# A third raw weight buffer, bias tables by products, and carried states four at a time, in one decoder layer step on one core

## The chip, the cores and the metric

The kernel runs on one core of a Trainium2 chip. Its engines have queues of their own and wait for each other by semaphores: TensorE (PE for matmuls, PEld for its weight loads), VectorE (DVE), ScalarE (ACT), GpSimd (POOL) and SyncE (SP), which here issues most DMA transfers. The metric is the device time of one execution in microseconds (us). TensorE's clock has two levels here, 2.4 and 1.2 GHz; the profile gives the granted clock of a stretch as a share of the upper one (PEclk).

## The reference, cut to what matters

One decoder layer step for a prompt of 256 tokens and 8 samples of 8 tokens, 320 columns in all, in float32:

```python
x = x + 0.5 * swiglu_ffn(rmsnorm(x, ffn1_norm), ffn1_w_in, ffn1_w_out)
h = rmsnorm(x, mix_norm)
z, xbc, dt_raw, q, kv, nsa_g, merge_g = jnp.split(h @ w_in_proj, cuts, axis=-1)
# state-space mixer: per sample and group, with the carried state h0
y_off = jnp.einsum('bclgn,bcgjpn->bclgjp', Cc, h_start) * decay_from_start[..., None]
h_final, h_start = lax.scan(step, h0, ...)      # h * decay + new state
# attention: compressed, selected and window keys, each with a bias by distance
s_c = jnp.einsum('bthgd,bnhd->bthgn', q, kc) + bias_qk(dist_c, bias_tab)
m = sig(gA) * (y_ssd @ w_branch_ssm) + sig(gB) * (y_nsa @ w_branch_attn);  x = x + m @ w_out
x = x + 0.5 * swiglu_ffn(rmsnorm(x, ffn2_norm), ffn2_w_in, ffn2_w_out)
```

`bias_tab` holds one bias for each of 32 buckets of distance and 16 heads. The samples read 2048 past tokens from paged caches, whose compressed keys and values (`kc`, `vc`) are computed in this step. A carried state has 64 rows by 128 columns for each of 32 heads; a group of eight heads of one sample is a 128 x 512 tile here, so there are 8 samples x 4 groups = 32 such tiles.

## The kernel before, in words

**The dense stream.** All big products take their weights in 245 blocks of up to eight K tiles (128 rows each, 1928 tiles in all). `w_load` (L300 to L308) lets SP load a block of 512 KB into one of `NRAW` = 2 buffers `wraw`. `w_hi` (L314) has ACT cast it to the high part `wh`; `w_lo` (L323) has DVE take the rest as the low part `wl` and then issues the next `w_load`, since the raw buffer is free from there on. `dense` (L328) runs three products for each K tile (L342 high x high, L343 low x high, L344 high x low), casts the high part of a later block at the first K tile of a block and the low part at `k == 1`. SP's queue is in order: a weight load stands behind whatever was issued before it, and with a wait of its own.

**The side work.** After each K tile `Sched.tick` adds `RATE[stage]` to a credit and lets generators take steps with it, so everything else stands between the K tiles of the dense stream in an order that is fixed when the program is written. `wait(n)` lets n ticks pass; `S.defer(n, f)` runs f after n ticks, from the front of a list.

**The stages**, in the time of the profiled execution: 0 to 390 the first feed-forward block, with the compression of the cached pages (`cmp_stream`) at its side; from 390 the projection `wproj`, first with `cmp_keys` (L717), `prompt_bias` (L839) and the prompt's attention, then from about 690 with the state-space mixer (`prompt_chunks`, `sample_chunks` L1747); from about 890 the samples' attention (`sample_attn`, `ring` of seven `KV` buffers) beside the last projections and branches; from about 1150 the second feed-forward block, whose norm takes its sums of squares with `Squares` (L347, products at L392).

**Bias.** In `cmp_stream` eight products (L638) make the bias of every head and distance, which POOL writes to DRAM (`trev`). At the end of the first feed-forward block SP issues, in this order: `xsp`, the two loads of `w1c` (L830), `scv` (L1178), three weight blocks, then the four loads of `prompt_bias` from `trev` into `blob` (L847), `flip` (L849), and the two small tables `tb` and `cb` (L837) in 16 loads, those of `cb` with single elements of 4 bytes. The product L855 needs `blob` and `flip`; L733 transposes the keys that `cmp_keys` has scaled on DVE (L726, L727), after `wait(4)`. `positions` (L599 to L603) has 16 one-column products (L602) twice in the program.

**Carried states.** `load_h` (L1726) loads state j into a ring of `NH` = 6 buffers, `AHEAD` = 4 states before it is used. In `sample_chunks`, for each even sample b, two products (L1772, 32 output rows each, in neighbouring groups of 32 rows) multiply the states of b and b + 1 by `cz`; then, for each state, POOL multiplies it by its decay (L1775), two products (L1778, L1779) make the new part, DVE adds it (L1780), the store of the state before is issued and then the load of state j + 4. Two samples make one step.

## Time and profile before

| what | value |
|---|---|
| three timed runs | 1389.57, 1389.86 and 1399.72 us, median 1389.86 |
| the profiled execution | 1398.44 us |
| its span, first to last instruction | 1396.4 us |
| busy: PE, PEld, DVE, ACT, POOL | 1329.4, 1177.7, 866.0, 592.8, 363.5 us |
| mean granted clock of PE in the span | 0.961 |
| DMA | 251.66 MB, mean 180 GB/s |

Busy time is a share of one span over stages with different limits. PE's busy time holds what it loses at the lower clock: an instruction at 1.2 GHz counts with its longer time. A view of the chain of waits follows the last instruction back, at each step to what released it. The timeline gives each instruction's start and length, and in brackets the idle time before it and its releaser. Windows sum up stretches.

### The profile page before, as it was taken

How to read it: one execution, taken by the hardware profiler on the slowest of the kernel's cores; microseconds unless marked ns; L12 is line 12 of the kernel's file. 1: busy time of each engine (PE TensorE's matmuls, PEld its weight loads, DVE VectorE, ACT ScalarE, POOL GpSimd, SP SyncE). 2: the span in 40 equal slices, each digit the busy share in tenths (PEclk: the TensorE clock that was granted, in tenths of full speed). 3: DMA queues.
4: the chain of work that ended last, by engine and by line, in shares of the span. 5: the costliest groups of instructions: out<-in, count | busy, mean ns of one | idle time of the engine just before them, and what ended most of it. 6: DMA issues, size and time to landing. Idle time of an engine off the chain costs nothing.

```text
span 1396.4 us, 28186 instructions
## 1 busy us (share of the span) xinstructions
PE 1329.4 (95%) x10583; PEld 1177.7 (84%) x10583; DVE 866.0 (62%) x1862; ACT 592.8 (42%) x1152; POOL 363.5 (26%) x616
## 2 busy tenths in 40 slices
PE   8999999999979999889989989799999999999998
PEld 7899999999858878677877756577677999999998
DVE  5577656655556457866567657657767766666533
ACT  4454543445434324446544343255555344333322
POOL 2222212222000216554444435233340010000000
PEclk9999999999989999889999999999999999999999
DMA  7556656666544325421177686778894443444453
GB/s 258 164 192 201 221 184 198 210 205 201 209 100 126 125 96 198 182 91 61 50 197 214 190 237 181 290 249 314 267 333 148 168 140 134 149 149 151 148 171 110
DMA packets 107041, 251.66 MB, mean 180 GB/s; under 512 B 23208, under 2 KB 49849, under 8 KB 104953
## 3 DMA queue, kind: packets, MB, share of 16 engines
q1 hardware_dynamic: 89946, 198.27, 44.2%
q0 software_dynamic: 16960, 51.61, 11.1%
q8 instruction: 83, 1.36, 0.4%
q14 instruction: 52, 0.43, 0.1%
HBM read 235.11 MB, written 23.10 MB: 185 GB/s over the span
## 4 chain that ended last, share of the span: by engine, by line
PE 72%; DVE 11%; DMA 5%; issue 4%; ACT 4%; SPq 2%; POOL 1%; POOLq 0%; ACTq 0%; DVEq 0%
PE ps_pd L342 18%; PE ps_pd L343 16%; PE ps_pd L344 16%; DVE wl L323 3%; PE ps_sc L671 2%; PE ps_sc L672 2%; PE ps_sc L681 2%; ACT wh L314 2%; PE ps_sc L1431 2%; DVE cvo L1198 2%; PE ps_po L1471 1%; DMA out_ssmS<-h 1%; PE ps_pt L1457 1%; PE ps_po L1319 1%; PE ps_sc L1270 1%
## 5 line engine op out<-in xcount | busy, mean ns | idle before, releaser
L323 DVE TENSOR_TENSOR wl<-wraw,wh 128x1024 fp32r<-128x1024 f32 (+1 forms) x245 | 302.0, 1233 | 266.9 <-ACT wh L314 266.4
L342 PE MATMUL ps_pd<-hh,wh 128*128 128x320 f32 x1320 | 452.5, 343 | 4.5 <-ACT hh L751 1.8
L343 PE MATMUL ps_pd<-hl,wh 128*128 128x320 f32 x1320 | 418.0, 317 | 1.6 <-DVE hl L450 1.4
L344 PE MATMUL ps_pd<-hh,wl 128*128 128x320 f32 x1320 | 417.2, 316 | 0.0
L314 ACT CAST wh<-wraw 128x1024 fp32r<-128x1024 f32 (+1 forms) x245 | 252.7, 1031 | 167.2 <-PE ps_pd L343 125.0
L342 PEld LDWEIGHTS ps_pd<-hh,wh 128*128 128x128 f32 x1320 | 257.4, 195 | 44.6 <-issue 32.8
L343 PEld LDWEIGHTS ps_pd<-hl,wh 128*128 128x128 f32 x1320 | 257.6, 195 | 10.2 <-issue 5.3
L344 PEld LDWEIGHTS ps_pd<-hh,wl 128*128 128x128 f32 x1320 | 256.5, 194 | 0.0
L342 PE MATMUL ps_pd<-ah,wh 128*128 128x320 f32 x352 | 109.4, 311 | 0.0
L344 PE MATMUL ps_pd<-ah,wl 128*128 128x320 f32 x352 | 108.7, 309 | 0.0
L343 PE MATMUL ps_pd<-al,wh 128*128 128x320 f32 x320 | 98.7, 309 | 0.0
L563 POOL DMA_DIRECT2D pg<-in_cache x136 | 74.3, 547 | 73.6 <-DVE pgl L575 30.6
L235 POOL TENSOR_SCALAR ah<-ff 128x320 fp32r<-128x320 f32 x44 | 20.1, 458 | 277.9 <-DVE ff L478 277.8
L575 DVE TENSOR_TENSOR pgl<-pg,pgh 128x512 fp32r<-128x512 f32 x128 | 82.4, 685 | 15.1 <-ACT pgh L568 14.9
L1384 POOL DMA_DIRECT2D KV<-in_cache x102 | 55.0, 539 | 104.3 <-PE ps_po L1471 68.5
L473 ACT ACTIVATE sg<-sg 128x320 f32<-128x320 f32 x44 | 20.8, 472 | 135.1 <-DVE sg L472 135.0
L568 ACT CAST pgh<-pg 128x512 fp32r<-128x512 f32 x128 | 72.6, 616 | 9.0 <-PE ps_sc L672 7.3
L671 PE MATMUL ps_sc<-pgh,w1h 128*128 128x256 f32 x256 | 68.6, 289 | 2.5 <-ACT pgh L568 2.5
L672 PE MATMUL ps_sc<-pgh,w1l 128*128 128x256 f32 x256 | 68.6, 288 | 0.0
L342 PEld LDWEIGHTS ps_pd<-ah,wh 128*128 128x128 f32 x352 | 66.1, 188 | 0.5
L344 PEld LDWEIGHTS ps_pd<-ah,wl 128*128 128x128 f32 x352 | 66.1, 188 | 0.0
L343 PEld LDWEIGHTS ps_pd<-al,wh 128*128 128x128 f32 x320 | 60.2, 188 | 0.0
(453 smaller groups left out, 2250.2 us busy)
## 6 DMA issues: line engine op xcount, KB each, us to landing
wraw<-in_wproj SPq DMA_DIRECT2D x77, 512.0 KB
KV<-in_cache POOLq DMA_DIRECT2D x102, 256.0 KB, 5.4
wraw<-in_w1in SPq DMA_DIRECT2D x44, 512.0 KB
wraw<-in_w2in SPq DMA_DIRECT2D x44, 512.0 KB
pg<-in_cache POOLq DMA_DIRECT2D x136, 128.0 KB, 4.1
pg<-in_cache SPq DMA_DIRECT2D x120, 128.0 KB
wraw<-in_w1out SPq DMA_DIRECT2D x16, 512.0 KB
h<-in_ssm SPq DMA_DIRECT2D x32, 256.0 KB
```

Of the source, the lines that this page charges most:

```text
L314: a.copy(h[:, :n], st["raw"][i][:, :n])
L323: v.tensor_tensor(l[:, :n], st["raw"].pop(i)[:, :n], st["hl"][i][0][:, :n], op=ALU.subtract)
L342: pe.matmul(out, wh[:, s], xh[:, kk, :], start=kk == 0, stop=False)
L343: pe.matmul(out, wh[:, s], xl[:, kk, :], start=False, stop=False)
L344: pe.matmul(out, wl[:, s], xh[:, kk, :], start=False, stop=kk == K - 1)
L563: e.dma_start(page(s, half)[:, i, :], I["cache"][ds(r, 1), :, 256 * c : 256 * c + 256].rearrange("o p f -> p (o f)"))
L568: a.copy(h[:, 8 * half : 8 * half + 8, :], page(s, half)[:, :, 64 * q : 64 * q + 64])
L575: v.tensor_tensor(l[:, 8 * half : 8 * half + 8, :], page(s, half)[:, :, 64 * q : 64 * q + 64], h[:, 8 * half : 8 * half + 8, :], op=ALU.su ...
L671: pe.matmul(ph, wh[:, j, :], h[:, :, j, :], start=q + j == 0, stop=False)
L672: pe.matmul(ph, wl[:, j, :], h[:, :, j, :], start=False, stop=False)
L681: pe.matmul(ph, wh[:, j, :], l[:, :, j, :], start=False, stop=q + j == 6)
L1384: e.dma_start(t[:, j, :], I["cache"][ds(r, 1), :, 512:1024].rearrange("o p f -> p (o f)"))
```

## The change

Four things are changed, and some counts beside them.

1. Three raw weight buffers in place of two; the low part is issued at the third K tile of a block (`k == 2`). The DMA scratch is halved from 8192 to 4096.
2. `tb` and `cb` no longer come from `trev` by 16 loads. In `cmp_stream`, after the loop that makes `trev`, 24 products (one for each of eight tokens and three groups of columns: 8, 63 and 1) with 33 rows of weights add them up in one PSUM tile; `relz` is `rel` spread with zeros between. `flip` is loaded there too. The four loads of `blob` are issued before `w1c`; `scv` is loaded later, at the fifth block of the projection. `cmp_keys` waits seven ticks instead of four.
3. Four carried states are multiplied at once, for b = 0 and b = 4, from a ring of eight buffers, loaded five ahead; the load is issued before the store. `xl` has 128 rows instead of 64, so that L1779 (now L1788) reads them all. The first `stage_b` of the samples stands six ticks later; `RATE[4]` is 0.88 instead of 0.85. `WS`, the wait at the start of the samples' attention, is 4 instead of 8.
4. `defer` sorts its list by what is left to wait; the squares before the second feed-forward block are deferred by 5 instead of 3.

```diff
-W0, W1, W2, W3, WS, EB = 3, 3, 6, 1, 8, 2
+W0, W1, W2, W3, WS, EB = 3, 3, 6, 1, 4, 2
-RATE = (0.59, 1.2, 0.9, 1.5, 0.85, 1.0, 1.0)
+RATE = (0.59, 1.2, 0.9, 1.5, 0.88, 1.0, 1.0)
     def defer(self, n, f):
-        self.later.append([n, f])
+        i = len(self.later)
+        while i and self.later[i - 1][0] > n:
+            i -= 1
+        self.later.insert(i, [n, f])
-    NRAW, SA = 2, 2
+    NRAW, SA = 3, 2
-                if k == 1:
+                if k == 2:
                     w_lo()
...
+        gcopy(relz[:, 7::8][:, 0:16], rel[:, 0:16])
+
+        p = bank("sc", (128, 72))
+        last = lambda t: oht[:, 6 - t : 7 - t] if t < 7 else oh[:, 2047:2048]
+        for o, n, src in ((0, 8, lambda t: oht[:, 7 - t : 15 - t]), (8, 63, lambda t: oh[:, 38 - t : 2048 - t : 32][:, 0:63]),
+                          (71, 1, last)):
+            for t in range(T):
+                pe.matmul(p[:, o : o + n], relz[:, 7 - t : 135 - t], src(t), start=t == 0, stop=t == T - 1)
+        a.copy(kcv[:, 2048:2120], p)
         release("oh")
+        sp.dma_start(flip, I["con"][:, C_KEEP : C_KEEP + 128])
...
-        yield from wait(4)
+        yield from wait(7)
...
-        flip = st["blob"][:, 4600:4728]
-        sp.dma_start(flip, I["con"][:, C_KEEP : C_KEEP + 128])
-        load_bias(tb, PAST, 8)
-        load_bias(cb, 31, 64, 32)
...
-        NH, AHEAD = 6, 4
+        NH, AHEAD = 8, 5
...
-            xl = sx.tile([64, 512], F32R, tag="xl", bufs=1, name="xl")
+            xl = sx.tile([128, 512], F32R, tag="xl", bufs=1, name="xl")
...
+                if q == 0:
+                    yield from wait(6)
                 stage_b(q, 2)
...
-                    if b % 2 == 0:
-                        for x_ in range(2):
-                            r = 32 * ((b + x_) % 4)
-                            pe.matmul(py[r : r + 32, :], cz[:, b + x_, :], pend["h", j + x_], start=b + x_ < 4,
-                                      stop=b + x_ >= 4)
+                    if b % 4 == 0:
+                        for x_ in range(4):
+                            r = 32 * x_
+                            pe.matmul(py[r : r + 32, :], cz[:, b + x_, :], pend["h", j + x_], start=b == 0, stop=b == 4)
...
+                    load_h(j + AHEAD)
                     store("outH")
                     pend["outH"] = O["ssmS"][b, :, 512 * q : 512 * q + 512], h0
-                    load_h(j + AHEAD)
...
-    early = chain(cmp_keys(), prompt_bias(), selector(), until("gates"), both(gates_rows(), decays()))
+    bias_ = prompt_bias()
+    next(bias_)
+    for c in range(2):
+        sp.dma_start(w1b[:, c], I["w1c"][:, c])
+    early = chain(cmp_keys(), bias_, selector(), until("gates"), both(gates_rows(), decays()))
...
+        if i == 4:
+            sp.dma_start(scv, I["sconv"])
...
-    sq = Squares(8, 3)
+    sq = Squares(8, 5)
```

Where the instructions stand shows in the order on each queue. SP, at the border of the first feed-forward block and the projection, before (`xsp` keeps the residual, `w1t` is `w1c`'s place):

```order
L305 DMA wraw<-in_wproj 128x1024 x4
L778 DMA xsp<-x 128x2560
L830 DMA w1t<-in_w1c 128x2048 x2
L1178 DMA scv<-in_sconv 128x576
L305 DMA wraw<-in_wproj 128x1024 x3
L847 DMA blob<-trev 64x4x256 x4
L849 DMA blob<-in_con 128x128
L837 DMA tb<-trev 16x8 x8
L837 DMA cb<-trev 16x64x1 x8
```

and after the change:

```order
L308 DMA wraw<-in_wproj 128x1024 x4
L794 DMA xsp<-x 128x2560
L859 DMA blob<-trev 64x4x256 x4
L1863 DMA w1t<-in_w1c 128x2048 x2
L308 DMA wraw<-in_wproj 128x1024 x6
L901 DMA blob<-in_con 48x432
```

The loads of `blob` stand four places earlier, ahead of `w1c`; the 16 loads of the tables are gone, and `scv` and `flip` stand elsewhere.

PE in the first feed-forward block, at the last product that makes `trev` (L638), before:

```order
L638 MATMUL ps_sc<-oht,rel 32x72
L342 MATMUL ps_pd<-hh,wh 128x320
L343 MATMUL ps_pd<-hl,wh 128x320
L344 MATMUL ps_pd<-hh,wl 128x320
L342 MATMUL ps_pd<-hh,wh 128x320
```

and after the change, three K tiles of the dense stream behind that product (now L644):

```order
L345 MATMUL ps_pd<-hh,wh 128x320
L346 MATMUL ps_pd<-hl,wh 128x320
L347 MATMUL ps_pd<-hh,wl 128x320
L656 MATMUL ps_sc<-oht 128x8 x8
L656 MATMUL ps_sc<-pg_119,oht 128x63 x8
L656 MATMUL ps_sc<-oht 128x1 x7
L656 MATMUL ps_sc<-pg_119,oht 128x1
L345 MATMUL ps_pd<-hh,wh 128x320
```

The 24 products stand in one piece between two K tiles.

PE in the first group of carried states, before (`h0` the states, `ps_po` the output that all samples of a group share):

```order
L1772 MATMUL ps_po_8452<-h0_8141,cz_8133 32x512
L1772 MATMUL ps_po_8452<-h0_8143,cz_8133 32x512
L1778 MATMUL ps_sc_8456<-xh_8391,bz_8395 128x512
L1779 MATMUL ps_sc_8456<-xl_8392,bz_8395 128x512
L1778 MATMUL ps_sc_8463<-xh_8391,bz_8395 128x512
L1779 MATMUL ps_sc_8463<-xl_8392,bz_8395 128x512
L342 MATMUL ps_pd_8411<-hh_4690,wh_8314 128x320
L343 MATMUL ps_pd_8411<-hl_4691,wh_8314 128x320
```

and after the change:

```order
L1782 MATMUL ps_po_8631<-h0_8152,cz_8144 32x512
L1782 MATMUL ps_po_8631<-h0_8154,cz_8144 32x512
L1782 MATMUL ps_po_8631<-h0_8156,cz_8144 32x512
L1782 MATMUL ps_po_8631<-h0_8158,cz_8144 32x512
L1787 MATMUL ps_sc_8637<-xh_8536,bz_8540 128x512
L1788 MATMUL ps_sc_8637<-xl_8537,bz_8540 128x512
L1787 MATMUL ps_sc_8644<-xh_8536,bz_8540 128x512
L1788 MATMUL ps_sc_8644<-xl_8537,bz_8540 128x512
L345 MATMUL ps_pd_8615<-hh_4720,wh_8478 128x320
L346 MATMUL ps_pd_8615<-hl_4721,wh_8478 128x320
```

Four states stand in a row where there were two; the next four follow after the new parts of four states. SP in the same group, where the second four states are loaded, before:

```order
L305 DMA wraw_8369<-in_wproj 128x1024
L1581 DMA abs_8417<-ascr_80 64x8x64
L305 DMA wraw_8425<-in_wproj 128x1024
L1726 DMA h0_8460<-in_ssm 128x512
L1679 DMA out_ssmS<-h0_8141 128x512
L1726 DMA h0_8468<-in_ssm 128x512
L1679 DMA out_ssmS<-h0_8143 128x512
L1726 DMA h0_8487<-in_ssm 128x512
L1679 DMA out_ssmS<-h0_8145 128x512
L1726 DMA h0_8495<-in_ssm 128x512
```

and after the change:

```order
L308 DMA wraw_8629<-in_wproj 128x1024
L1733 DMA h0_8641<-in_ssm 128x512
L1733 DMA h0_8648<-in_ssm 128x512
L1686 DMA out_ssmS<-h0_8152 128x512
L1733 DMA h0_8662<-in_ssm 128x512
L1686 DMA out_ssmS<-h0_8154 128x512
L1733 DMA h0_8670<-in_ssm 128x512
L1686 DMA out_ssmS<-h0_8156 128x512
L1681 DMA ecb_8684<-ascr_80 64x4x128 x2
L1733 DMA h0_8706<-in_ssm 128x512
L1686 DMA out_ssmS<-h0_8158 128x512
L1733 DMA h0_8714<-in_ssm 128x512
```

The load of a state stands ahead of a store instead of behind it; states 6 and 7 of a group stand right before and right behind the first store.

## Rows read from the trace of the kernel before

**Rows 1.** The page, part 1: busy time, share and instructions of each engine.

```profile
PE 1329.4 (95%) x10583; PEld 1177.7 (84%) x10583; DVE 866.0 (62%) x1862; ACT 592.8 (42%) x1152; POOL 363.5 (26%) x616
```

**Rows 2.** Timeline of PE; in brackets idle time before, and its releaser.

```profile
395.58 1.11 PE L733 MATMUL ps_sc<-con,kcv 128*128 128x128 f32 x4 [2.45 <-DVE kcv L727]
...
411.84 2.05 PE L855 MATMUL ps_sc<-blob 128*128 128x512 f32 x2 [4.44 <-DMA blob<-in_con]
...
717.49 1.12 PE L1637 MATMUL ps_pt<-abs,xdt 64*64 64x64 f32 x16 [5.42 <-POOL abs L1627]
...
807.04 0.80 PE L1778 MATMUL ps_sc<-xh,bz 128*128 128x512 f32 x1 [4.42 <-ACT btok L1608]
...
902.60 1.06 PE L1431 MATMUL ps_sc<-KV,qbs 64*32 64x512 f32 x1 [5.97 <-DVE ms L1444]
...
1159.26 0.38 PE L392 MATMUL ps_pt<-ones,sq 128*128 128x1 f32 x2 [1.30 <-ACT sq L365]
```

**Rows 3.** Chain of waits, three windows: start, length, what.

```profile
404.55 7.21 DMA blob<-in_con
...
704.40 8.33 DMA wraw<-in_wproj
...
889.02 12.84 DMA KV<-in_cwin
```

**Rows 4.** Timeline of SP from 360 to 404.

```profile
374.67 0.33 SPq L778 DMA_DIRECT2D xsp<-x  x1
...
400.58 3.61 SPq L847 DMA_DIRECT2D blob<-trev  x4
```

**Rows 5.** Waits of SP's queue: total, times, longest, all in us.

```profile
SPq L305 <- DVE wl L323: 816.5, 207, 14.1
...
SPq L1726 <- DMA out_ssmS<-h: 43.0, 15, 6.1
...
SPq L1178 <- DVE hf L447: 11.2, 1, 11.2
```

**Rows 6.** Windows: busy time and instructions of five engines, PEclk, DMA share.

```profile
395.60:406.00 10.40, 10.40 (x55) 8.92 (x56) 5.67 (x7) 4.48 (x8) 0.00 (x0) 0.84 0.61 166
...
406.00:412.00 6.00, 1.56 (x10) 1.32 (x10) 1.23 (x1) 1.70 (x3) 0.00 (x0) 0.77 0.69 138
...
412.00:424.00 12.00, 12.00 (x49) 8.19 (x49) 0.00 (x0) 3.15 (x6) 0.00 (x0) 0.83 0.62 83
...
718.00:724.00 6.00, 6.00 (x35) 5.88 (x32) 2.89 (x8) 1.37 (x2) 4.08 (x2) 0.57 0.37 111
...
808.00:814.00 6.00, 6.00 (x16) 2.69 (x17) 1.87 (x4) 0.00 (x0) 1.67 (x2) 0.67 1.01 287
...
903.00:911.00 8.00, 8.00 (x37) 5.03 (x36) 3.76 (x12) 4.73 (x11) 0.54 (x1) 0.50 0.73 294
```

**Rows 7.** Windows behind the first one-column products.

```profile
55.60:60.40 4.80, 4.80 (x34) 4.80 (x33) 2.36 (x5) 0.77 (x2) 2.74 (x6) 0.71 0.77 201
...
60.40:64.40 4.00, 4.00 (x16) 4.00 (x17) 1.92 (x4) 0.09 (x1) 0.97 (x2) 0.50 0.88 305
```

**Rows 8.** Chain of waits: the two runs of one-column products.

```profile
55.64 4.70 PE ps_po L602 x32
...
229.13 4.17 PE ps_po L602 x32
```

**Rows 9.** PE: pairs of carried states (timeline), eight score products (chain).

```profile
735.64 1.05 PE L1772 MATMUL ps_po<-h,cz 128*32 128x512 f32 x4
...
741.58 1.05 PE L1772 MATMUL ps_po<-h,cz 128*32 128x512 f32 x4
...
919.75 1.02 PE ps_sc L1431 x16
```

**Rows 10.** Chain of waits from 815 to 830.

```profile
819.25 5.57 DMA h<-in_ssm
...
827.97 0.15 PE ps_pd L343
```

More of the change, by code (lines that the diff above doesn't have):

```diff
@@ L513, in step_kernel @@
         sp.dma_start(x[:, 2 * i : 2 * i + 2, :], I["xT"][:, 2 * i : 2 * i + 2, :])
-        if i == 1:
+        if i % 2:
             w_load()
@@ L521, in step_kernel @@
     kraw = kT.rearrange("p b (a d) -> p b a d", a=2)
+    tb, cb, flip = kcv[:, 2048:2056], kcv[:, 2056:2120], kcv[:, 2120:2248]
     kss = cp.tile([128, NB, 2], F32, name="kss")
@@ L524, in step_kernel @@
     pew = cp.tile([128, 2], F32, name="pew")
-    rel = fp.tile([NBK + 1, 32], F32, name="rel")
     held, LAG, numbers = [], 1, {}
@@ L621, in cmp_stream @@
         yield
+        oht = fp.tile([NBK + 1, TL - 2048 + 168], F32, tag="hid", bufs=1, name="oht")
+        rel = oht[:, TL - 2048 : TL - 2016]
+        relz = oht[:, TL - 2016 :]
+        g.memset(relz, 0.0)
         g.memset(rel, -BIG)
@@ L625, in cmp_stream @@
         oh = raws["oh"][: NBK + 1]
-        oht = fp.tile([NBK + 1, TL - 2048], F32, tag="hid", bufs=1, name="oht")
         sp.dma_start(oh, I["oh"][:, 0:2048])
-        sp.dma_start(oht, I["oh"][:, 2048:])
+        sp.dma_start(oht[:, 0 : TL - 2048], I["oh"][:, 2048:])
         sp.dma_start(con[:, 128:], I["con"][:, 128:C_KEEP])
@@ L637, in cmp_stream @@
             p = bank("sc", (32, NT))
-            pe.matmul(p[:, :n], rel, oh[:, k : k + n] if k < 2048 else oht, start=True, stop=True)
+            pe.matmul(p[:, :n], rel, oh[:, k : k + n] if k < 2048 else oht[:, 0 : TL - 2048], start=True, stop=True)
             tv = tp.tile([32, NT], F32, tag="sq", name="tv")
@@ L814, in step_kernel @@
     pq = q0.enter_context(tc.tile_pool(name="pq", bufs=1))
-    tb = pq.tile([128, 8], F32, name="tb")
-    cb = pq.tile([128, 64], F32, name="cb")
     vst = pq.tile([128, 256], F32, name="vst")
@@ L827, in bl, with load_bias @@
         return st["blob"][:, o : o + m * n].rearrange("p (a b) -> p a b", a=m)
-    for c in range(2):
-        sp.dma_start(w1b[:, c], I["w1c"][:, c])
     tr0 = trev[0:16, :]
-    def load_bias(dst, k0, n, step=1):
+    def load_bias(dst, k0, n):
         for t in range(T):
-            src = bass.AP(tensor=tr0.tensor, offset=tr0.offset + 7 - t + k0, ap=[[TL, 16], [step, n]])
+            src = bass.AP(tensor=tr0.tensor, offset=tr0.offset + 7 - t + k0, ap=[[TL, 16], [1, n]])
             sp.dma_start(dst[t :: T, :], src)
@@ L1177, in step_kernel @@
     scv = cvs.tile([128, 24, NB, 3], F32, name="scv")
-    sp.dma_start(scv, I["sconv"])
     v.tensor_scalar(cwh, par[:, P_CW : P_CW + 120], 0.5, None, op0=ALU.mult)
@@ L1744, in parts @@
             pend["hl"] = xh, xl, bz
-            pend["lo"] = xl, xde[:64], xh[:64]
+            pend["lo"] = xl, xde, xh
         def sample_chunks():
@@ L1778, in sample_chunks @@
                     pe.matmul(p, bz[:, b, :], xh, start=True, stop=False)
-                    pe.matmul(p, bz[:64, b, :], xl, start=False, stop=True)
+                    pe.matmul(p, bz[:, b, :], xl, start=False, stop=True)
                     v.tensor_tensor(h0, h0, p, op=ALU.add)
+                    load_h(j + AHEAD)
                     store("outH")
                     pend["outH"] = O["ssmS"][b, :, 512 * q : 512 * q + 512], h0
-                    load_h(j + AHEAD)
                     if b % 2:
@@ L2149 @@
     from concourse.bass_utils import run_bass_kernel_spmd
-    nc = bacc.Bacc("TRN2", target_bir_lowering=False, num_devices=1, dynamic_dma_scratch_size=8192)
+    nc = bacc.Bacc("TRN2", target_bir_lowering=False, num_devices=1, dynamic_dma_scratch_size=4096)
     arrays = {f"in_{k}": x for k, x in _layout(inputs).items()}
```

## The prediction

> **What bounds the kernel now.** I read the busy time first: PE is busy for 1329.4 of the span's 1396.4 us [rows 1]. So PE is the bound, and only two things can be won: the 67.0 us in which it sits idle, and what its clock loses. The gaps of PE's timeline come next. Five of the largest stand at places the change touches, 2.45, 4.44, 5.42, 4.42 and 5.97 us, and a small one of 1.30 [rows 2], 24.0 us in all. Then the windows: behind such a gap PE works on, but at a granted clock of 0.57, 0.67 or 0.50 [rows 6], that is partly or wholly at 1.2 GHz. A window of t us busy at clock c loses t x (1 - c). Last the chain of waits and SP's queue, for what stands behind each gap [rows 3 to 5]. A stall is thus worth its idle time and a dip of the clock behind it.
>
> The sum is made against the profiled execution, 1398.44 us (span 1396.4 and 2.0 around it). That is 8.6 above the median of 1389.86 and near the highest of the three runs shown; I take the sum's difference off the median.
>
> **Border of the first feed-forward block (keys and bias).** SP issues `xsp` at 374.67; `w1c` and `scv` follow, `scv` waits 11.2 us for DVE's last `hf` [rows 4, 5], and so the three weight blocks behind it are late and `blob` goes out at 400.58 [rows 4]. PE waits for `blob` 4.44 us, until 411.84 [rows 2], on a transfer of 7.21 [rows 3]. In the changed order `blob` stands right behind `xsp`, some 25 us earlier; even if it had to wait there for the same 11.2 us and took 7.21 to land, it would be there by about 394, long before its product, and the table loads behind it are gone. All 4.44 go. What it pushes back is `w1c`, by four issues that took 3.61 [rows 4]; its readers come much later. The wait for the scaled keys is 2.45; the transposes move by five K tiles, 5 x 3 products x 0.15 [rows 10] = 2.25, so 0.2 stays. Removed: 6.7. The clock behind both lost 10.40 x 0.16 + 1.56 x 0.23 + 12.00 x 0.17 = 4.1 [rows 6]. I take 2.8 of it, since a short wait or a late weight block can still stand there. **Gain 9.5 (6.7 to 10.8).**
>
> **Third raw buffer.** A weight load waits for DVE's low part, 816.5 us in 207 times [rows 5]; mostly this is SP running ahead, and costs nothing. It costs where loads come late to PE. At 712 PE waits 5.42 for a chain that holds a weight transfer of 8.33 us, begun at 704.40 only because a buffer came free there [rows 2, 3]. With a third buffer that load may start a block earlier, 8 K tiles x 3 x 0.15 = 3.6 us at the least, more when side work stands between. Gap and dip (6.00 x 0.43 = 2.6) are worth 8.0 [rows 6]. The cast, a POOL multiplication and so on stay in the chain. I take 6 (3.6 to 8). At 802 PE waits 4.42, dip 6.00 x 0.33 = 2.0 [rows 2, 6]. SP was held there by loads of states that waited for the store of the state two before, 43.0 us in 15 times [rows 5]. With eight buffers, five loaded ahead, the store to wait for was issued a state earlier, so most of these waits shrink, and the block has a buffer more. I take 5 (0 to 6.4). The low part one K tile later costs DVE nothing and PE nothing as long as two blocks are split ahead; bounded by one K tile, 0.45, at the few places where it is late. Elsewhere there are 67.0 - 24.0 = 43 us of small gaps; some are waits for weights. I take 1.5 (-2 to 4). **Gain 12.5 (1.6 to 18.4).**
>
> **Four states at once.** Two products of 32 output rows, in 4 records, take 1.05 in the timeline; eight products of the same form in the samples' scores, 16 records, take 1.02 [rows 9]. So products on different parts of the array run side by side, and four should last as long as two. 16 pairs become 8 fours: 8 x 1.0 = 8.0. The other end is 0, if four in one set of rows don't overlap. The scores' products use 64 rows and 32 columns of the array, these 128 and 32, so four of these fill what eight of those do; I take the full 8.0 since that row is the nearest. `xl` with 128 rows costs nothing on PE; its subtraction on DVE stays one instruction for each of four groups. **Gain 8 (0 to 8.4).**
>
> **What the fours wait for.** A four needs states j to j+3. States 6 and 7 of a group are issued one or two steps before the second four. A state takes 5.57 us to land [rows 10]; from one pair to the next, a step, it was 5.94 us [rows 9]; SP has other work between. That is close. At one end nothing is late; at the other each of the seven later fours waits a little over one us, 8 in all. **Cost 2 (0 to 8)**, nearer the lower end since a step is the longer of the two.
>
> **Start of the samples' attention.** PE waits 5.97 and then runs 8.00 us at clock 0.50, 4.0 lost [rows 2, 6], behind a transfer of window rows that took 12.84 [rows 3] while the queues were full. The stage's later cache loads move back by some seven K tiles, which leaves room for this transfer; against it, two of the cache loads now also wait for the last stores of states. I take a **gain of 4 (-6 to 10)**.
>
> **Squares.** The wait is 1.30 [rows 2]; two more K tiles are 0.9. The sorted list lets later items not hold shorter ones. **Gain 1.5 (0 to 3).**
>
> **The new products.** 24 products in float32 are 48 records. The nearest rows: 32 records of one column took 4.70 and 4.17 [rows 8], 0.147 and 0.130 each, so 6.2 to 7.1; 63 columns are few enough to be hidden by the weight loads of those rows. Behind the first such run the clock fell though PE never idled: 0.71 over 4.80 us and 0.50 over 4.00, with PE busy throughout [rows 7], 1.4 + 2.0 = 3.4 lost. By these rows the price lies between 6.2 and 10.5; I take 8.5, as part of the 1.4 is in the 4.70 already. POOL's copy, ACT's copy and the memset hide beside the dense stream: ACT and POOL are busy for less than half of the span (592.8 and 363.5 us). Before, 16 loads cost PE nothing but SP's queue.
>
> The Trainium skill, "TensorE: Matmul & The Clock Gate", section "Why this matters for your kernels", says to keep TensorE busy without idle gaps between bursts to hold the full clock. By it a piece of 24 products without a gap would lose no clock, and the price would be 6.2 in place of 8.5. The row above shows a fall without any gap, and I go by the row.
>
> **Sum.** 9.5 + 12.5 + 8 + 4 + 1.5 = 35.5 won; 8.5 + 2 = 10.5 paid; 25 us net. The profiled frame gives 1398.4 - 25 = 1373.4, the median 1389.86 - 25 = **1365**.
>
> **Rivals.**
> - *The weight loads stay late.* The third buffer frees a load from DVE, but SP's queue is in order; where a store, `ecb` or `ab` stands ahead with a wait of its own, the load goes out when it did. For it: the loads of states held SP for 43.0 us [rows 5]. Against: these waits shrink too. Then the 12.5 are about 0: 1365 + 12.5 = 1378.
> - *The samples' attention starts later.* Cache loads behind the last stores lengthen the gap of 5.97 by one landing of about 5.6 in place of shortening it, with a dip of the same size: 4 becomes -9, and 1365 + 13 = 1378.
> - *Slower: the fours stand and wait.* Seven fours come after the first. If the last state of each lands w us late, each costs w and a dip of about 2.3 (the mean of 2.6 and 2.0). Without the 2 us assumed above 27 are won; 7 x (w + 2.3) passes them from w = 1.6. At w = 3 it is 37, and the time 1390 - 27 + 37 = 1400. For it: landing 5.57 against a step of about 6. Against: SP issues the load a state earlier than it did, and ahead of the store.
> - *Fours that run as two pairs* (the change does not do what it says): 8 us are gone, 1373. That lies inside the range of the forecast.
> - *No clock is lost by the new products*, as the rule above would have it: 1389.86 - 27.3 = 1363, a chance of 0.1 within the forecast's.
>
> **How the numbers follow.** Of a measurement of this kernel a difference under 1% (14 us) can't be told from none, as the three runs shown lie 10 us apart. Chances: forecast 0.64, with a range of its own of about 1350 to 1376 from the bounds above (they don't all fall on one side); late weight loads 0.14; late samples' attention 0.12; waiting fours 0.06; all gains at their upper ends, about 1345, 0.04. 1% below is 1376, so both rivals at 1378 stand at the border: about 0.4 of each is faster. Faster 0.64 x 0.97 + 0.04 + 0.26 x 0.4 = 0.76; slower by over 1% (1404) 0.04; the rest, 0.20, is within. The range leaves out the upper ends, the fours and the outer parts of the two rivals: 1347 to 1384.
>
> **What the profile after would show.** Gaps before L855's and L733's successors near 395 and 411 gone or under 0.5; gap near 712 under 2; loads of states in SP's waits well under 43.0; 64 records of carried states in about 10 us, eight pieces of about 1 us; the new products as 48 records in 6 to 7 us behind a window with clock under 0.8; PE's busy time down by about 10, its idle time by 15. Wrong it would be made by a new gap at each four, by a longer wait for the window rows before the first score product, or by new waits of ACT's casts on weight transfers in the second feed-forward block, where DMA now has a buffer more to fill.

## The result, and the profile after

The changed kernel takes 1374.1 us (median of five runs, 1370.72 to 1381.27), the kernel before in the same comparison 1395.63 (1389.57 to 1399.72): a ratio of 0.985, with a 95% interval of 0.9814 to 0.9886. It is 21.5 us faster where the forecast was 25, and the time lies inside the range of 1347 to 1384. The forecast's own figure, 1365, is 9.1 below it; 5.8 of these come from the kernel before, whose median is 1395.63 here and was 1389.86 in the three runs that the forecast started from. The profiled execution took 1381.27 with a span of 1379.3, against 1396.4 before, 17.1 less.

First the page's row of PE, which answers to [rows 1]: busy time fell by 11.0 us and idle time by 6.1, to 60.9.

```profile
PE 1318.4 (96%) x10631; PEld 1179.7 (86%) x10631; DVE 869.7 (63%) x1862; ACT 591.7 (43%) x1153; POOL 365.2 (26%) x618
```

Idle time fell by less than the gaps of [rows 2] held. Their successors in the timeline of PE: the transposes of the keys (L749, before L733), the product of `blob` (L863, before L855) and the samples' first `stage_b` (L1644, before L1637) have no wait any more, and the product of the carried states L1782 has a new one of 3.92. The second set of score products waits 1.20 where it waited 5.97, and inside the first set there is a new wait of 1.74.

```profile
408.59 0.60 PE L749 MATMUL ps_sc<-con,kcv 128*128 128x128 f32 x4
...
417.75 1.02 PE L863 MATMUL ps_sc<-blob,kcv 128*128 128x512 f32 x2
...
727.79 0.68 PE L1644 MATMUL ps_pt<-abs,xdt 64*64 64x64 f32 x16
...
785.81 3.31 PE L1782 MATMUL ps_po<-h,cz 128*32 128x512 f32 x4 [3.92 <-DMA h<-in_ssm]
...
882.22 1.09 PE L1438 MATMUL ps_sc<-KV,qbs 64*32 64x512 f32 x14 [1.74 <-DMA KV<-in_cache]
...
887.36 1.06 PE L1438 MATMUL ps_sc<-KV,qbs 64*32 64x512 f32 x1 [1.20 <-DVE ms L1451]
```

PE's waits, in the order total, times, longest: those for states (L1782) were 0.3 before and are 8.9; the products of the new parts (L1787) wait 5.1 for DVE's additions, which the forecast's sum does not have.

```profile
PE ps_po L1782 <- DMA h<-in_ssm: 8.9, 6, 3.9
...
PE ps_sc L1787 <- DVE h L1789: 5.1, 6, 2.3
```

And SP's waits, which answer to [rows 5]: that of the loads of states (L1733) for stores is down from 43.0, that of the weight loads (L308) up from 816.5.

```profile
SPq L308 <- DVE wl L326: 883.3, 212, 11.6
...
SPq L1733 <- DMA out_ssmS<-h: 27.0, 14, 4.6
```

The clock in windows (busy time and instructions of PE, PEld, DVE, ACT, POOL, then PEclk, DMA share and GB/s). The stretch of the new products (52 to 68, with [rows 7] as its like) is at 0.68, a stretch at the start (30 to 44) at 0.63, and behind the first scores (884 to 897, [rows 6]) it is 0.51 as it was 0.50.

```profile
30.00:44.00 14.00, 12.21 (x39) 7.98 (x39) 4.87 (x8) 3.60 (x6) 2.51 (x5) 0.63 0.54 174
...
52.00:68.00 16.00, 15.87 (x86) 15.44 (x86) 4.44 (x6) 3.39 (x7) 2.07 (x5) 0.68 0.19 63
...
884.00:897.00 13.00, 11.80 (x49) 8.02 (x49) 5.75 (x16) 5.71 (x13) 4.32 (x8) 0.51 0.86 318
```

To see where the time went I use one measure for all kernels. Every trace holds all 5784 products of the dense stream, 3 for each of the 1928 K tiles, in one order; so the start of K tile n is the same point of the work in each. The table gives the time from one such point to the next (0 is the first product, the last column reaches to the end of the span): in us for the kernel before, and as the difference to it for the others. Side work can move from one stretch to the next, so stretches are cut where little does.

| kernel | 0-40 | 40-90 | 90-520 | 520-640 | 640-880 | 880-1120 | 1120-1280 | 1280-end |
|---|---|---|---|---|---|---|---|---|
| before | 32.1 | 35.0 | 292.9 | 96.4 | 234.8 | 252.8 | 146.3 | 297.7 |
| changed | +4.2 | +9.0 | -1.9 | -9.0 | -0.4 | -17.4 | -1.1 | -0.8 |
| a_again | +4.4 | +9.3 | -2.4 | -9.8 | +2.0 | -17.1 | -5.1 | -0.8 |
| a_tables_dma | +6.2 | +0.9 | -1.2 | -8.9 | -0.6 | -16.5 | -5.5 | -2.3 |
| a_spread | +6.4 | +0.7 | -1.3 | -6.7 | +1.5 | -19.7 | -5.7 | -0.8 |
| a_two_raw | +7.3 | +9.0 | -2.7 | -9.0 | -3.6 | -9.4 | -2.5 | -2.3 |
| a_pairs | +0.0 | +9.2 | -1.9 | -8.9 | -1.9 | -10.3 | -3.9 | +0.8 |
| a_no_wait6 | +4.7 | +9.1 | -1.8 | -8.9 | +0.5 | -0.0 | -6.3 | +0.7 |
| a_ws8 | +7.2 | +11.0 | -1.8 | -9.0 | +1.4 | -28.7 | +1.5 | -2.1 |
| a_dma_bias4 | -0.5 | -1.6 | -3.4 | -9.2 | -1.9 | -26.7 | -5.1 | -0.8 |
| b_three_raw | -0.4 | -0.0 | -2.5 | -0.3 | -2.8 | +0.1 | -3.5 | -1.0 |
| b_border | +0.4 | -0.0 | -2.0 | -3.0 | +2.2 | +0.1 | -0.2 | -0.3 |
| b_xl128 | -0.6 | -0.0 | -5.2 | +1.4 | -4.2 | -5.1 | -0.3 | +0.3 |
| b_bias4 | +1.0 | -1.6 | -2.0 | -0.7 | -2.5 | -4.9 | +0.3 | -0.4 |

The names are those of the experiments below; a_again is the changed kernel once more, and shows how far one execution lies from another: up to 4 us in a stretch, 2.6 in all. Each row is one execution. In the changed kernel two stretches lose (13.2 us up to K tile 90) and two win (9.0 at the border, 17.4 in the state-space stage and the start of the samples' attention).

These 17.4 are for the most part work and not waiting. Windows over K tiles 880 to 1120, first before, then after the change:

```profile
699.60:952.40 252.80, 231.72 (x1726) 169.82 (x1724) 161.77 (x361) 102.33 (x222) 101.01 (x110) 0.95 0.72 227
...
701.70:937.10 235.40, 215.63 (x1757) 166.82 (x1755) 168.26 (x362) 102.30 (x225) 101.53 (x110) 0.96 0.76 244
```

PE's busy time falls by 16.1, some 3 of it by the clock, and its idle time by only 1.3, from 21.1 to 19.8.

### The profile page after: what moved, and what is told of

It reads as the page before. It is cut to its first block, busy times and chain, and to the rows that moved or that the text cites. A ratio compares the mean times of both kernels' runs of the same rounds, so it can differ in the third digit from the quotient of the medians.

```text
span 1379.3 us, 28261 instructions
## 1 busy us (share of the span) xinstructions
PE 1318.4 (96%) x10631; PEld 1179.7 (86%) x10631; DVE 869.7 (63%) x1862; ACT 591.7 (43%) x1153; POOL 365.2 (26%) x618
## 5 line engine op out<-in xcount | busy, mean ns | idle before, releaser
L345 PE MATMUL ps_pd<-hh,wh 128*128 128x320 f32 x1320 | 449.5, 341 | 6.2 <-ACT hh L767 2.2
L326 DVE TENSOR_TENSOR wl<-wraw,wh 128x1024 fp32r<-128x1024 f32 (+1 forms) x245 | 305.2, 1247 | 181.2 <-ACT wh L317 180.9
L345 PEld LDWEIGHTS ps_pd<-hh,wh 128*128 128x128 f32 x1320 | 257.0, 195 | 43.9 <-issue 28.9
L345 PE MATMUL ps_pd<-ah,wh 128*128 128x320 f32 x352 | 109.5, 311 | 0.0
L345 PEld LDWEIGHTS ps_pd<-ah,wh 128*128 128x128 f32 x352 | 66.2, 188 | 0.5
```

Of the source, the lines that this page charges most:

```text
L326: v.tensor_tensor(l[:, :n], st["raw"].pop(i)[:, :n], st["hl"][i][0][:, :n], op=ALU.subtract)
L345: pe.matmul(out, wh[:, s], xh[:, kk, :], start=kk == 0, stop=False)
```

## The experiments

Names with a_ start from the changed kernel, with b_ from the kernel before. Times are medians; ratios are to runs of the kernel before on the same chip, with their 95% intervals. Theory 1 is the forecast's list with the sizes that the changed kernel's trace shows; theory 2, for the last four, is what the first eight runs had left of it.

**a_tables_dma and a_spread: what the products cost.** The first drops the products and loads the tables as before, behind `w1c`; the second steps the schedule between pieces of four.

```diff
-                pe.matmul(p[:, o : o + n], relz[:, 7 - t : 135 - t], src(t), start=t == 0, stop=t == T - 1)
-        a.copy(kcv[:, 2048:2120], p)
...
         sp.dma_start(w1b[:, c], I["w1c"][:, c])
+    load_bias(tb, PAST, 8)
+    load_bias(cb, 31, 64, 32)
```

```diff
                 pe.matmul(p[:, o : o + n], relz[:, 7 - t : 135 - t], src(t), start=t == 0, stop=t == T - 1)
+                if t % 4 == 3:
+                    yield
```

> The changed kernel, with the two small tables again by 16 loads (issued behind the w1c loads) and without the 24 products; all else as changed. Theory 1 (the products cost PE about 9 us with the clock they lose, and the 16 loads cost nothing where they now stand): the 9 us by which the changed kernel falls behind between K tiles 50 and 65 are gone, nothing is lost at the border, time 1365. Rival (the 16 loads were a good part of the stall at the border, in SP's queue ahead of the weights): the 9 us come back there, as waits of ACT's cast for a weight transfer between K tiles 540 and 600, time 1370 to 1375.

> The changed kernel with the 24 products in six pieces of four, a step of the schedule between them; this also moves the rest of the page compression by six steps. Theory 1 (the clock falls behind the long piece of products whose weight loads, not their columns, set the pace): no window at clock 0.5 near 57 to 67 us, cost of the products 6 to 7 instead of about 10, time 1370. Rival (the price is in the products themselves): K tiles 50 to 90 lose the same 9 to 10 us, time 1374.

Measured: a_tables_dma 1368.28, ratio 0.9823 (0.9775 to 0.9871); a_spread 1374.08, ratio 0.9882 (0.9852 to 0.9912). From K tile 40 to 90 the products in one piece cost 9.0 us; with loads it is 0.9, in pieces 0.7. The 16 loads cost nothing at the border here, -8.9 as with products. Theory 1 holds at both places in the traces. The medians show less: that of a_spread is the rival's 1374 and the changed kernel's own (1374.1), and the interval of a_tables_dma overlaps that of a_again below. The timeline of PE in a_spread: each piece is 8 records in 1.05 to 1.14, and dense products stand between.

```profile
59.03 1.05 PE L656 MATMUL ps_sc<-oht 33*128 33x8 f32 x8
...
61.97 1.13 PE L656 MATMUL ps_sc<-pg,oht 33*128 33x63 f32 x8
```

Its window from 52 to 68 is at full clock, where the changed kernel has 0.68 with about as much of the time busy:

```profile
52.00:68.00 16.00, 15.78 (x106) 13.81 (x105) 6.93 (x10) 3.87 (x6) 2.78 (x6) 1.00 0.29 96
```

Over the whole stretch from K tile 40 to 90 the account closes. Windows of the kernel before, the changed kernel and a_spread, and what follows in a_spread:

```profile
40.40:75.40 35.00, 35.00 (x222) 32.89 (x221) 19.74 (x30) 14.49 (x25) 8.31 (x16) 0.90 0.54 170
...
44.90:88.90 44.00, 43.87 (x270) 41.48 (x270) 19.73 (x30) 14.80 (x26) 8.36 (x17) 0.84 0.37 120
...
46.80:82.50 35.70, 35.48 (x240) 31.86 (x239) 15.99 (x25) 13.44 (x23) 7.39 (x15) 1.00 0.41 125
...
82.50:87.00 4.50, 4.50 (x23) 4.50 (x23) 3.50 (x5) 0.70 (x2) 0.00 (x0) 0.62 0.59 192
```

Busy time x (1 - clock) is 3.5 us before, 7.0 in the changed kernel and none in a_spread; without it PE is busy for 31.5, 36.9 and 35.5. So of the 9 us some 5.4 are the products' own and 3.5 the clock; in pieces the products still cost some 4, where theory 1 had 6 to 7. a_spread shows only 0.7 because the dip that the kernel before has here, behind the one-column products [rows 7], comes in a_spread just after K tile 90 (0.62 from 82.5 to 87): its schedule has moved them by six steps.

**a_two_raw and b_three_raw: the third raw buffer, taken away and alone.**

```diff
-    NRAW, SA = 3, 2
+    NRAW, SA = 2, 2
...
-                if k == 2:
+                if k == 1:
```

b_three_raw is the reverse of this in the kernel before, with the halved DMA scratch.

> The changed kernel with two raw weight buffers and the low part at k == 1, the third early weight load gone. Theory 1 (the third buffer brings 6 us at the place of the 712 gap and more in the state-space stage, and costs 4.4 us at the start, where its early load stands before the others): K tile 40 comes about 4 us earlier than in the changed kernel, the stretch of K tiles 880 to 1080 takes 6 to 12 us more, time 1376 to 1382. Rival (the third buffer brings nothing, since loads wait in order in SP's queue): that stretch is the same within 2 us, time 1370.

> The kernel before with three raw buffers, the low part at k == 2 and the halved scratch, nothing else changed. Theory 1 (the third buffer by itself brings about 8 us in the state-space stage): the gap of 5.42 at 712 falls below 2, the gap of 4.42 at 802 below 3, the stretch of K tiles 880 to 1120 is 6 to 10 us shorter, time 0.993 to 0.995 of before. Rival (it pays only with the larger ring, whose loads wait less in SP's queue): both gaps stay within 1 us, ratio 0.998 to 1.002.

Measured: a_two_raw 1383.19, ratio 0.9933 (0.9902 to 0.9963); b_three_raw 1389.07, ratio 0.9961 (0.9933 to 0.999). Taken away, K tiles 880 to 1120 take 8 us more, as theory 1 had it, 4.5 of them up to K tile 1060 and the rest at the first scores; but the start did not come back (+7.3), so the early load is not what costs there. Alone, the buffer brings some 5 us, and not where theory 1 put them: the wait of `stage_b` is still 4.8, and near 802, where L1778 waited 4.42 for ACT's btok [rows 2], PE now waits 3.8 for a state. PE's waits in b_three_raw:

```profile
PE ps_po L1772 <- DMA h<-in_ssm: 5.3, 2, 3.8
...
PE ps_pt L1637 <- POOL abs L1627: 4.8, 1, 4.8
```

**b_border: only the order at the border.** The loads of `blob` ahead of `w1c`, the tables' behind it, `scv` later, seven ticks for the keys; two raw buffers, no products.

```diff
+    bias_ = prompt_bias()
+    next(bias_)
     for c in range(2):
         sp.dma_start(w1b[:, c], I["w1c"][:, c])
+    load_bias(tb, PAST, 8)
+    load_bias(cb, 31, 64, 32)
```

> The kernel before with only the order at the border changed: the four loads of the bias for the prompt and flip ahead of w1c, the tables' 16 loads behind w1c, scv at the fifth projection block, cmp_keys waiting seven ticks. Two raw buffers, pairs, no products. Theory 1 (the stall at the border comes from where blob and the keys stand, not from the tables' loads or the buffers): K tiles 520 to 640 are 9 us shorter, as in all traces of changed kernels, all other stretches within 3 us, ratio 0.993 to 0.995. Rival (the 16 loads, still on SP there, hold weight blocks): the gain at the border is below 5 us, ratio 0.997.

Measured: 1390.94, ratio 0.9974 (0.9951 to 0.9998), and only 3.0 us in the stretch. Neither old gap is there, but a new one of 4.28 stands at 400.68, at the product of the squares (L1873), which waits for ACT. The chain of waits there shows why: SP issues the 16 table loads (L835) one after the other, and the weight block behind them lands last.

```profile
396.68 0.92 SPq L835
...
397.64 0.66 SPq L835
...
398.42 4.12 DMA wraw<-in_wproj
```

The rival is right for two buffers: the loads hold a weight block. With three (a_tables_dma) or without the loads (a_two_raw) the border wins its 9 us. So the gain is the order's, on condition of one of the other two edits: a third buffer or no table loads.

**a_pairs: fours or pairs.**

```diff
-                    if b % 4 == 0:
-                        for x_ in range(4):
+                    if b % 2 == 0:
+                        for x_ in range(2):
```

> The changed kernel with the carried states multiplied in pairs instead of fours, ring of eight and five ahead kept. Theory 1 (four products side by side last as long as two): 8 us more of PE's time on these products, time 1382 if nothing else moves. Rival (what the fours save they give back by waiting for their last states, 8.9 us in the trace of the changed kernel): those waits fall below 3 us, time 1374 to 1376.

Measured: 1377.57, ratio 0.9905 (0.9871 to 0.9939), between the two theories; the interval overlaps that of a_again (0.9856 to 0.9929). PE's waits for states fall to 4.3 in two places:

```profile
PE ps_po L1782 <- DMA h<-in_ssm: 4.3, 2, 3.7
```

Theory 1 does not hold: with these waits the 64 records of the states' products take 22.5 us here, and 26.7 in the changed kernel. K tiles 880 to 1120 take 7 us more than in the changed kernel, but only 1.9 of that stand up to K tile 1060, in the state-space stage; 6.9 stand from 1100 to 1120, among the samples' scores, behind a wait of 2.54 for a cache load and a dip of the clock, where no product of the states is left (from 1060 to 1100 it is 1.8 less). So this run does not show that the fours win anything.

**a_again and a_dma_bias4: beside each other, and the bias loads in four pieces.** In the changed kernel SP's timeline shows what the wait of 3.92 at 781.9 stands behind: 16 loads of the samples' bias in one piece, and the load of the state after them.

```profile
765.89 11.32 SPq L1400 DMA_DIRECT2D bias<-trev  x16
...
779.89 0.42 SPq L1733 DMA_DIRECT2D h<-in_ssm  x1
```

```diff
                     early_bias()
+                if EB <= i < EB + 4:
+                    bias_part(i - EB)
```

`early_bias` then only makes the tiles, and `bias_part(k)` issues four of the 16 loads. a_dma_bias4 has this and the tables by loads.

> The changed kernel unchanged, beside the others on one chip. Theory 1 (the products cost it 9 us): 8 to 10 us above the kernel with the tables by loads, of the run before; rival (what differs between executions at the start and in the attention covers that): within 4 us of it. Between its two traces the stretch of K tiles 0 to 40 may differ by up to 7 us, since it was -0.1 to 7.3 in the five traces so far, with the same code there in three of them.

> The changed kernel with the tables by 16 loads and no products, as in the run before, and with the 16 loads of the samples' bias (L1400) issued in four pieces of four, behind the third to the sixth chunk of the prompt's states, instead of in one piece. Theory 1 (the second four of group 1 waits 3.9 us because SP issues the bias for 11.3 us ahead of the loads of states): that wait falls below 1 us, with the dip of the clock behind it, and the stretch of K tiles 960 to 1040 is 4 to 6 us shorter, time 1363 on the scale on which the run before gave 1368. Rival (the states are late by their stores, which hold the ring): PE's waits for states stay at 7 to 9 us in all, time 1368.

Measured in one comparison, in which the kernel before has a median of 1394.0: a_again 1379.17, ratio 0.9893 (0.9856 to 0.9929), so that the change wins 14.8 us here and 21.5 in the first comparison; a_dma_bias4 **1356.53**, ratio 0.9731 (0.9693 to 0.9769), 22.6 us below the changed kernel. By the ratios a_again lies 9.8 us above a_tables_dma, as its theory 1 has it, but the two were not run in one comparison and the intervals overlap. In a_dma_bias4 the wait at the second four of group 1 is 1.4, above the 1 that theory 1 allowed, but the time is below its 1363. In the trace, taken of its fastest execution (1348.97), PE's waits for states are 3.6 in all:

```profile
PE ps_po L1777 <- DMA h<-in_ssm: 3.6, 5, 1.4
```

By the table the 29.7 us between their spans are 4.9 at the start, 10.9 for the products, 9.6 from K tile 880 to 1120 and 4.3 elsewhere. Nothing in the two edits explains the 4.9 at the start; what goes with it is said at the end of the next section.

**b_bias4: the same pieces in the kernel before.**

> The kernel before with the 16 loads of the samples' bias (L1393) in four pieces of four, behind the third to the sixth chunk of the prompt's states. Theory 2 (PE's gap of 4.42 at 802 comes from the bias loads, which hold SP from 789.6 to 800.1 ahead of a weight block): the gap falls below 1 us, K tiles 960 to 1040 are 5 to 8 us shorter with the clock's dip, ratio 0.994 to 0.996. Rival (the forecast's view: loads of states that wait for the store of two states before hold SP, and the buffers are too few): gap within 1.5 us of 4.42, ratio 0.998 to 1.001.

Measured: 1387.85, ratio 0.9965 (0.9937 to 0.9993). The gap at 802 [rows 2] is gone, though the loads of states still wait for their stores 41.6 us (43.0 in [rows 5]). Theory 2 holds for the gap: the bias loads made it, not the stores. In SP's timeline of the kernel before they stand right ahead of two weight loads, the first at 800.84; below it the wait in b_bias4.

```profile
789.60 10.51 SPq L1393 DMA_DIRECT2D bias<-trev  x16
...
SPq L1730 <- DMA out_ssmS<-h: 41.6, 17, 5.7
```

**b_xl128: the low part on 128 rows, alone.**

```diff
-            xl = sx.tile([64, 512], F32R, tag="xl", bufs=1, name="xl")
+            xl = sx.tile([128, 512], F32R, tag="xl", bufs=1, name="xl")
...
-                    pe.matmul(p, bz[:64, b, :], xl, start=False, stop=True)
+                    pe.matmul(p, bz[:, b, :], xl, start=False, stop=True)
```

> The kernel before with one edit: the low part xl of the decayed inputs has 128 rows instead of 64, so that L1779 multiplies all rows of bz like L1778 (the product then also holds low part times low part). Theory 2, formed on the traces (two products of unlike shape, 128 x 128 and 64 x 128 of the array, do not overlap; of one shape they do): the products of L1778 and L1779 start 0.23 to 0.34 us apart instead of 0.43, their 64 take 17 to 18 us instead of 28.4, the stretch of K tiles 880 to 1080 is 10 to 12 us shorter, ratio 0.992. Rival (the forecast's view, that xl's rows cost nothing, and the shorter products come from the fours or the ring): 0.43 as before, ratio 0.999 to 1.001.

Timelines of PE, first before, where the four products of two states start 0.43 apart and the dense stream goes on 1.73 after the first:

```profile
768.58 0.50 PE L1778 MATMUL ps_sc<-xh,bz 128*128 128x512 f32 x1
...
769.01 0.50 PE L1779 MATMUL ps_sc<-xl,bz 64*128 64x512 f32 x1
...
769.45 0.50 PE L1778 MATMUL ps_sc<-xh,bz 128*128 128x512 f32 x1
...
769.88 0.50 PE L1779 MATMUL ps_sc<-xl,bz 64*128 64x512 f32 x1
...
770.31 0.42 PE L342 MATMUL ps_pd<-hh,wh 128*128 128x320 f32 x1
```

and in b_xl128, where they start 0.34 and 0.23 apart:

```profile
770.64 0.50 PE L1778 MATMUL ps_sc<-xh,bz 128*128 128x512 f32 x1
...
770.98 0.40 PE L1779 MATMUL ps_sc<-xl,bz 128*128 128x512 f32 x1
...
771.21 0.39 PE L1778 MATMUL ps_sc<-xh,bz 128*128 128x512 f32 x1
...
771.44 0.40 PE L1779 MATMUL ps_sc<-xl,bz 128*128 128x512 f32 x1
...
771.68 0.31 PE L342 MATMUL ps_pd<-hh,wh 128*128 128x320 f32 x1
```

Measured: 1389.17, ratio 0.9972 (0.9938 to 1.0005), which is not clear of noise and short of the 0.992 expected; the products themselves show it. Start to start, and without waits, the 64 products take 18.4 us instead of 28.4, as theory 2 has it; from K tile 880 to 1120 only 5.1 of these 10 are left. The pairs take back some of the rest: idle time before them rose from 0.3 to 2.8, and the 64 records themselves, within which a pair can wait for its second state, from 19.0 to 22.9. It is so in the other traces too: 27.7 to 28.9 us with 64 rows (b_bias4, b_border, b_three_raw), 17.1 to 19.7 with 128 (all nine of the changed and the a_ kernels).

**a_no_wait6: without the six ticks ahead of the samples' first `stage_b`.**

```diff
-                if q == 0:
-                    yield from wait(6)
```

> The changed kernel without the six ticks ahead of the samples' first stage_b. Theory 2 (these six ticks take away the gap of 5.42 at 712, which the third buffer does not: it is 4.8 with three buffers alone): a gap of 4 to 5.5 us with POOL's abs as its releaser comes back at the product of stage_b near K tile 908, and the time is 3 to 8 us above the changed kernel, about 0.993 of before. Rival (the third buffer covers it): no gap above 1 us there, time within 3 us of the changed kernel's, 0.985 to 0.989.

Measured: 1395.24, ratio 0.9973 (0.9942 to 1.0005): nearly all that the change wins is gone. The gap is back with three raw buffers, and at the first scores there are longer ones than in the changed kernel; the window behind them is at 0.50 for 18 us.

```profile
720.42 1.12 PE L1644 MATMUL ps_pt<-abs,xdt 64*64 64x64 f32 x16 [5.21 <-POOL abs L1634]
...
880.00:898.00 18.00, 13.57 (x57) 6.50 (x57) 4.66 (x15) 5.00 (x12) 4.34 (x9) 0.50 0.84 334
```

The gap is theory 2's. The loss is larger than the 3 to 8 us expected; the rest stands at the first scores with their longer waits, and how these follow from the six ticks no run here separates.

**a_ws8: `WS` = 8 again.**

```diff
-W0, W1, W2, W3, WS, EB = 3, 3, 6, 1, 4, 2
+W0, W1, W2, W3, WS, EB = 3, 3, 6, 1, 8, 2
```

> The changed kernel with WS = 8 as before: the first scores of the samples' attention stand four ticks later in the schedule. Theory 2 (at the start of the stage PE waits for transfers whatever stands there; four K tiles more cover part of it): the waits of 1.7 and 1.2 us near 880 shrink by up to 2 us, the end moves by -3 to +3 us. Rival (the shorter wait is what made the gap of 5.97 smaller): a gap of 4 us or more comes back there, 4 to 8 us slower.

Measured: 1377.71, ratio 0.9879 (0.9831 to 0.9926), as the changed kernel. PE's first wait at the scores is 2.08, none is 4 or more; in this one trace K tiles 880 to 1120 are 11 us shorter than in the changed kernel's (side work that moves to the next stretch, 2.6 longer, is a part of it), and the first 90 are 5 us longer. So the shorter `WS` is not what made the gap of 5.97 smaller.

## Why the prediction was right, point by point

The time and its sign were right, but in part by luck, as the sum's terms erred against each other: 11.3 us that it did not have stand against states that cost 7.4 where the two terms for them had 6 won. Of the signs named for the profile, PE's busy time (11.0 less), the gaps near 395, 411 and 712 and SP's waits came as said. Idle time fell by 6.1 and not by 15, the 64 records of the states took 17.7 and not about 10, and the 48 new records some 8 and not 6 to 7.

- **Border, 9.5 won:** 9.0 measured. The step was right that `blob` and the keys are what stalls; the transfer of 7.21 that it read as that of `blob` is the one of `flip` (`blob<-in_con` [rows 3]), which moved as well. Idle time fell by 7.5 there, more than the 6.7 of the sum; the clock gave back only some 0.4 of the 2.8, as it dips behind two waits of about 1 us that are left. That the 16 loads cost nothing but queue time holds only with a third buffer (b_border).
- **Third buffer, 12.5 won:** mis-sized and misplaced. Alone it gave 5 us; inside the change its absence costs 8 from K tile 880 to 1120. The 6 at 712 belong to the six ticks, to which the forecast gave no price at all (a_no_wait6; b_three_raw keeps 4.8 of 5.42, and in a_two_raw, with the ticks and two buffers, the gap is gone). The 5 at 802 rested on the stores that hold SP; b_bias4 shows that the 16 bias loads did, and in the changed kernel the stall came back there as a wait for a state, 3.92.
- **Fours, 8 won:** the mechanism was right where the states are there. The first four of each group lasts as long as a pair; the second comes in pieces. The timeline of PE shows both in the first group:

```profile
735.43 1.06 PE L1782 MATMUL ps_po<-h,cz 128*32 128x512 f32 x8
...
736.43 0.50 PE L1787 MATMUL ps_sc<-xh,bz 128*128 128x512 f32 x1
...
744.69 1.05 PE L1782 MATMUL ps_po<-h,cz 128*32 128x512 f32 x2
...
746.00 1.70 PE L1782 MATMUL ps_po<-h,cz 128*32 128x512 f32 x4 [0.26 <-DMA h<-in_ssm]
...
747.98 1.05 PE L1782 MATMUL ps_po<-h,cz 128*32 128x512 f32 x2 [0.28 <-DMA h<-in_ssm]
```

- **What the fours wait for, 2 paid (0 to 8):** this step failed. The four first fours take 1.0 each, from the first start to what follows them; the four second ones take 4.3, 10.5, 2.8 and 5.1, that is 18.7 more than they would undisturbed: 8.9 of idle time in six waits, and the rest because products whose states come one by one no longer run side by side (in the second group also at the lower clock). All eight take 26.7 where the pairs before took 19.3 with their waits; with the bias loads in pieces (a_dma_bias4) it is 18.1. The rival of waiting fours had the mechanism, but at four places instead of seven and with one dip of the clock (0.66 from 781 to 791) instead of seven.
- **`xl` on 128 rows, "costs nothing on PE":** this step failed too, the other way. It gains: 28.4 us start to start in the kernel before are 17.1 in the changed one (32 + 32 products, waits left out), 11.3 us that the sum did not have. They cover most of what the states' terms were short of. From K tile 880 to 1120 the parts lean on each other: undone one by one, the buffer and the six ticks cost 8 and 17 us, more than the 17.4 that stand there in all (5.2 of the 17 come back in the next stretch).
- **Products, 8.5 paid (6.2 to 10.5):** 9.0 to 9.3 in five of the six traces with the products in one piece, 11.0 in a_ws8. In the changed kernel PE is busy for 15.87 of 16.00 us from 52 to 68 at a clock of 0.68. The Trainium skill, "TensorE: Matmul & The Clock Gate", section "Why this matters for your kernels", ties the loss to idle gaps, and by it the price would have been 6.2; this trace does not agree.
- **Samples' attention, 4 won:** about nothing that can be seen apart from its neighbours. The wait of 5.97 became 1.74 and 1.20; the clock behind lost 11.80 x 0.49 = 5.8 instead of 4.0, which leaves 1.2.
- **Squares, 1.5 won:** the gap of 1.30 has gone, but PE now waits 1.82 for ACT's `hh` at a dense product just ahead of them (L345, at 1140.20). The last stretch is 0.8 shorter.
- **Not in the sum:** 4.2 us at the start. Of the nine traces of the changed and the a_ kernels seven lose 4.2 to 7.3 there, a_pairs and a_dma_bias4 nothing; a_two_raw loses it without the early load. It goes with a longer wait for a load and a dip of the clock behind it: in the changed kernel 1.2 us more of idle time up to K tile 40 and 3.4 more lost to the clock. In six of the seven PE waits 1.8 to 4.1 for the load of `oh` at the first product that makes `trev` (L644; in a_two_raw it waits 3.09 for DVE just before), and then runs at the lower level for 7 to 17 us; in a_pairs and a_dma_bias4 that wait is 0.93 and 0.34, and the clock stays up. Timeline and windows of PE, the changed kernel (its window stands in the section on the result) and then a_pairs:

```profile
31.79 0.70 PE L644 MATMUL ps_sc<-pg,oht 33*32 33x320 f32 x2 [1.88 <-DMA pg<-in_oh]
...
31.86 0.69 PE L644 MATMUL ps_sc<-pg,oht 33*32 33x320 f32 x2 [0.93 <-DMA pg<-in_oh]
...
30.00:44.00 14.00, 13.07 (x70) 8.98 (x68) 7.42 (x11) 5.87 (x11) 3.52 (x7) 1.00 0.55 185
```

  Why that load lands late in some executions is open.

## What to carry to other kernels

A queue that is in order makes every long run of small loads a stall for whatever comes behind it: here 16 loads on SP cost a weight block at the border and a state in the middle, and cutting the run in the middle in four won as much in the kernel before as a further buffer (0.9965 and 0.9961). Products that are to run side by side win only when all their inputs are there: fours that waited for their last states took longer than pairs. When a change moves work, price each edit of the diff, the dull ones too: without a wait of six ticks nearly all of this gain was gone, and a tile with twice the rows shortened its products by 11 us. And compare traces at points of the work that both kernels share, cut into idle time, clock and the rest; ends alone could not tell half of these runs apart.

## What the runs showed of the hardware

- Two products that use the array in unlike shapes follow each other slower than two of one shape: 0.43 us from start to start for 128 x 128 and 64 x 128 in turn, 0.23 for 128 x 128 throughout, both of 512 columns at full clock. The Trainium skill, "TensorEngine Tiling (Array Packing)", section "Tiling Modes", says that a change of tiling mode drains the engine; the traces agree, and by them 0.2 us a change is an estimate of the price for these two shapes (0.43 - 0.23).
- The granted clock fell with PE busy throughout. In all six traces with the 48 small records in one piece it fell to the lower level while the piece ran and stayed there for 7 to 10 us (0.68 from 52 to 68 in the changed kernel). In the one trace with the same records in six pieces between dense products it did not (1.00 in the same window of a_spread), and fell only behind the 32 one-column products.
